# A column sum over 32,768 rows: the tile scheduler's ring against a hand-synchronised ring with loops

## Chip, cores and metric

The kernel runs on one core of one Trainium2 chip. The metric is the device time of one execution in microseconds; the time of the kernel before is the median of seven runs. A profile of one further execution gives the instructions of each engine, the DMA packets with their start, length and size, and every landing of a transfer. VectorE (DVE in the profile), TensorE (PE, with PEld for its weight loads), ScalarE (ACT), GpSimd (POOL) and SyncE (SP) are the engines; 16 DMA engines move the data. All times here are microseconds unless marked ns.

## The reference

```python
def setup_inputs():
    batch, seq, dim = 32, 1024, 2048
    return {"grad_output": np.random.randn(batch, seq, dim).astype(np.float32)}

def reference(grad_output):
    return np.sum(grad_output, axis=(0, 1)).astype(np.float32)
```

The input is 32,768 rows of 2,048 float32, which is 268.4 MB; the output is one row of 2,048. The work is one addition for each number that is read.

## The kernel before

The input is seen as 32,768 rows. They are taken in blocks of 128 x m rows: partition p gets m neighbouring rows, so that a block is m "single rows" of 128 partitions x 2,048 columns, 1 MB each, and 256 single rows make up the input. Below, a row is such a single row. A load of m rows takes from each partition one contiguous piece of m x 8 KB.

Three buffers matter. `ring` has room for 24 rows (192 KB of each partition), `head` for one, and `ones` is a column of ones with which a matmul sums over the partitions. PSUM holds the sums, one bank for each piece of columns: three pieces of 512 (`LEFT`) and two of 256 (`RIGHT`). The third number of a piece is the group of 32 partitions in which its sum stands: 1, 2 and 3 for the left pieces, 0 and 1 for the right ones. `add` (lines 65 to 71) issues one matmul for each piece of a row.

`PLAN` (line 14) is the list of the loads: 27 tiles of 8 rows, then 7, 6, 6, 5, 4, 2, -2, 2, -2. For a positive number VectorE adds. It first adds the running sum to the new tile (line 114), then folds the tile (line 93): a tile of 8 rows is folded to 4 while fewer than 23 tiles have been added (`N_WIDE`, `WIDE`), and to a single row behind that, by halving. For a negative number the rows are not folded: TensorE sums them straight into PSUM (lines 104 to 107). Behind the last positive tile stand three filler matmuls into a bank of their own (line 120). Then the running sum goes to PSUM (line 121).

`LAST` = (2, 1) are the last three rows. They are loaded in two halves of columns, first the left 1,536 columns of both loads, then the right 512, into a place of their own, and TensorE sums them with the stop flag on the last (lines 125 to 133). Lines 134 to 138 copy the five sums from PSUM to `res`, which lies in `head`: ScalarE the pieces 0, 2 and 4, VectorE 1 and 3. Line 139 sends `res` out.

All loads are issued by SP (line 85), one after the other in the order of the program. A load into a place of the ring waits until the last reader of that place is done; these waits, and all others between engines, are put in by the tile framework. The places follow one another in the ring and start again at 0 when a tile doesn't fit behind the last one; for the tiles of 8 that makes three places.

Lines 51 and 52 issue 60 drains on VectorE at the start of its program. Line 53 sets `ones`, line 54 is a copy on ScalarE that has no use but to load its table.

Of the kernel before, what the change touches and what calls it, by code (L numbers as in the profile page):

```python
# [1 line left out]

# [4 lines left out]

P = 128
RING = 24  # L10

PLAN = (8,) * 27 + (7, 6, 6, 5, 4, 2, -2, 2, -2)
LAST = (2, 1)

N_WIDE = 23
WIDE = 4
DRAINS = 60
FILLERS = 3  # L20

LEFT = ((0, 512, 1), (512, 512, 2), (1024, 512, 3))
RIGHT = ((1536, 256, 0), (1792, 256, 1))


@with_exitstack
def kernel(
    ctx: ExitStack,
    tc: tile.TileContext,
    grad_output: bass.AP,  # L30
    out: bass.AP,
):
    nc = tc.nc
    fp32 = mybir.dt.float32
    D = out.shape[-1]
    flat = grad_output.rearrange("b s d -> (b s) d")
    R = flat.shape[0]
    assert (1 + sum(abs(m) for m in PLAN) + sum(LAST)) * P == R

    const_pool = ctx.enter_context(tc.tile_pool(name="const", bufs=1))  # L40
    psum_pool = ctx.enter_context(tc.tile_pool(name="psum", bufs=1, space=bass.MemoryType.PSUM))

    ring = const_pool.tile([P, RING * D], fp32)
    head = const_pool.tile([P, D], fp32)
    ones = const_pool.tile([P, 1], fp32)
    warm = const_pool.tile([1, 1], fp32)
    res = head[0:1, :]

    for _ in range(DRAINS):
        nc.vector.drain(fusable=False)
    nc.gpsimd.memset(ones[:], 1.0)  # L53
    nc.scalar.copy(out=warm[:], in_=ones[0:1, :])  # L54

    sums = {}
    for b, (lo, n, g) in enumerate(LEFT + RIGHT):
        bank = psum_pool.tile([P, 512], fp32, tag=f"ps{b}", name=f"ps{b}")  # L60
        sums[lo] = bank[32 * g : 32 * g + 1, :n]
    junk = psum_pool.tile([P, 512], fp32, tag="junk", name="junk")
    started = set()

    def add(at, pieces, base=0, stop=False):
        for lo, n, g in pieces:
            x = at + lo - base
            nc.tensor.matmul(  # L68
                sums[lo], lhsT=ones[:], rhs=ring[:, x : x + n], start=(lo not in started), stop=stop
            )  # L70
            started.add(lo)

    row = pos = 0

    def take(m):
        nonlocal pos
        if pos + m > RING:
            pos = 0
        at = pos
        pos += m  # L80
        return at

    def load(first, m, dst, lo=0, hi=D):
        src = flat[first : first + P * m].rearrange("(p m) d -> p m d", p=P)[:, :, lo:hi]
        nc.sync.dma_start(out=dst.rearrange("p (m d) -> p m d", m=m), in_=src)  # L85

    def rows(at, m):
        return ring[:, at * D : (at + m) * D]

    def fold(at, height, to):  # L90
        while height > to:
            k = min(height - to, height // 2)
            nc.vector.tensor_add(out=rows(at, k), in0=rows(at, k), in1=rows(at + height - k, k))  # L93
            height -= k

    load(row, 1, head[:])
    row += P
    run = height = None
    n_fold = 0
    for m in PLAN:  # L100
        at = take(abs(m))
        load(row, abs(m), rows(at, abs(m)))
        row += P * abs(m)
        if m < 0:
            for j in range(-m):
                add((at + j) * D, LEFT + RIGHT)
            continue
        to = min(m, WIDE if n_fold < N_WIDE else 1)
        if n_fold == 0:
            nc.vector.tensor_add(out=rows(at, 1), in0=rows(at, 1), in1=head[:])  # L110
        else:
            to = min(to, height)
            fold(run, height, to)
            nc.vector.tensor_add(out=rows(at, to), in0=rows(at, to), in1=rows(run, to))  # L114
        n_fold += 1
        fold(at, m, to)
        run, height = at, to
        if n_fold == sum(m > 0 for m in PLAN):
            for _ in range(FILLERS):
                nc.tensor.matmul(junk[0:1, :], lhsT=ones[:], rhs=rows(at + m - 1, 1)[:, :512], start=True, stop=True)  # L120
    add(run * D, LEFT + RIGHT)

    at = take(sum(LAST)) * D
    cut = RIGHT[0][0]
    for lo, hi, pieces in ((0, cut, LEFT), (cut, D, RIGHT)):
        first = row
        for i, m in enumerate(LAST):
            n = hi - lo
            load(first, m, ring[:, at : at + m * n], lo, hi)
            first += P * m  # L130
            for j in range(m):
                add(at, pieces, base=lo, stop=(i == len(LAST) - 1 and j == m - 1))
                at += n
    for k, (lo, n, g) in enumerate(LEFT + RIGHT):
        if k in (0, 2, 4):
            nc.scalar.copy(out=res[:, lo : lo + n], in_=sums[lo])  # L136
        else:
            nc.vector.tensor_copy(out=res[:, lo : lo + n], in_=sums[lo])  # L138
    nc.sync.dma_start(out=out[None, :], in_=res)


# [1 line left out]
_INS = ['grad_output']  # L143
_OUTS = [((2048,), 'float32')]


# [23 lines left out]
```

## Time and profile before

| what | value |
|---|---|
| median of 7 runs | 630.68 |
| all runs | 630.46, 630.62, 630.64, 630.68, 630.69, 631.35, 631.50 |
| the profiled execution's own time | 631.31 |
| its span, first to last instruction | 629.2 |
| VectorE busy | 544.0 (86%), 89 instructions |
| TensorE busy | 16.7 (3%), 86 instructions |
| DMA, over the span | 268.46 MB, 427 GB/s |
| packets | 6164 |
| 8-row loads, issue to landing, median | 29.9 |
| the output row's issue | 626.32 |

The span is what the profile's clock shows between the first and the last instruction; the device time is 2.1 longer in the profiled execution. The busy share of an engine is an average over the whole span. "Idle before" in a group of instructions is the time for which its engine stood still just ahead of them, with what ended it. The chain of waits is followed back from the last instruction: at each step to what released it, or to the instruction before it on its engine.

### The profile page before, as it was taken

To read this page: it belongs to the slowest core of one execution; us is meant where nothing else is said; L and a number is where in the kernel's file an instruction comes from. 1 tells how busy PE (TensorE), PEld (TensorE's weight loads), DVE (VectorE), ACT (ScalarE), POOL (GpSimd) and SP (SyncE) were. 2 spreads that over 40 slices of the span, in tenths; PEclk is the share of its full clock that TensorE was granted. 3 is DMA by queue.
4 is the path that set the end of the run, shared out by engine and by line. 5 is a ranking of instruction groups with operands and counts; after the bars stand their busy time and mean duration, and the time that the engine had idled before them with its cause. 6 is when DMAs were issued, how large, how long until landed. Compare 5 with 4: busy or idle time off the path is not lost.

```text
span 629.2 us, 484 instructions
## 1 busy us (share of the span) xinstructions
PE 16.7 (3%) x86; PEld 3.7 (1%) x86; DVE 544.0 (86%) x89; ACT 3.0 (0%) x5; POOL 0.3 (0%) x5
## 2 busy tenths in 40 slices
PE   0000000000000000000000000000000000000046
PEld 0000000000000000000000000000000000000001
DVE  0349888889888898888998888988899999999994
ACT  0000000000000000000000000000000000000000
POOL 0000000000000000000000000000000000000000
PEclk9999999999999999999999999999999999999998
DMA  9999999999999999999999999999999999999995
GB/s 400 417 450 417 450 417 450 421 446 425 442 425 442 429 437 433 433 437 429 442 425 450 417 454 412 454 412 458 408 458 408 458 408 433 430 447 406 426 427 231
DMA packets 6164, 268.46 MB, mean 427 GB/s; under 512 B 657, under 2 KB 657, under 8 KB 1425
## 3 DMA queue, kind: packets, MB, share of 16 engines
q1 hardware_dynamic: 6162, 268.45, 98.8%
q14 instruction: 2, 0.02, 0.0%
HBM read 268.44 MB, written 0.01 MB: 427 GB/s over the span
## 4 chain that ended last, share of the span: by engine, by line
DMA 60%; DVE 37%; PE 2%; issue 0%; another core or an unknown queue 0%; SPq 0%; ACT 0%; DVEq 0%
DMA ring<-in_grad_output_dram 60%; DVE ring L114 19%; DVE ring L93 18%; PE ps L68 2%; SPq L85 0%; ACT head L136 0%; DVEq L114 0%
## 5 line engine op out<-in xcount | busy, mean ns | idle before, releaser
L93 DVE TENSOR_TENSOR ring<-ring 128x8192 f32<-128x8192 f32 (+3 forms) x53 | 324.1, 6116 | 1.8
L114 DVE TENSOR_TENSOR ring<-ring 128x8192 f32<-128x8192 f32 (+1 forms) x33 | 216.4, 6559 | 49.7 <-DMA ring<-in_grad_output_dram 49.3
L68 PE MATMUL ps<-ring,ones 128*1 128x512 f32 (+1 forms) x80 | 13.9, 647 | 608.9 <-DMA ring<-in_grad_output_dram 608.9
L110 DVE TENSOR_TENSOR ring<-ring,head 128x2048 f32<-128x2048 f32 x1 | 2.3, 2293 | 25.4 <-DMA ring<-in_grad_output_dram 25.4
L68 PEld LDWEIGHTS ps<-ring,ones 128*1 128x1 f32 x80 | 3.2, 89 | 619.5 <-issue 615.3
L138 DVE COPY head<-ps 1x512 f32<-1x512 f32 (+1 forms) x2 | 1.1, 548 | 5.1 <-PE ps L68 5.1
L136 ACT COPY head<-ps 1x512 f32<-1x512 f32 (+1 forms) x3 | 1.5, 507 | 622.6 <-PE ps L68 622.4
L120 PE MATMUL junk<-ring,ones 128*1 128x512 f32 x6 | 2.7, 592 | 0.4 <-DMA ring<-in_grad_output_dram 0.4
L54 ACT ACT_TABLE_LOAD x1 | 1.3, 1283 | 0.7 <-PEq L154 0.7
L120 PEld LDWEIGHTS junk<-ring,ones 128*1 128x1 f32 x6 | 0.4, 83 | 2.3 <-issue 1.4
L54 ACT COPY warm<-ones 1x1 f32<-1x1 f32 x1 | 0.2, 191 | 0.0
L154 POOL MEMSET const-bfloat16-1.0<- 128x1 bf16 x1 | 0.1, 103 | 0.0
L154 POOL MEMSET const-uint8-127<- 128x1 uint8 x1 | 0.1, 103 | 0.0
L53 POOL MEMSET ones<- 128x1 f32 x1 | 0.1, 100 | 0.3 <-POOLq L154 0.3
L154 POOL MEMSET const-float32-0.0<- 128x1 f32 x1 | 0.1, 99 | 0.2 <-issue 0.2
L154 POOL MEMSET const-float32-1.0<- 128x1 f32 x1 | 0.1, 99 | 0.0
## 6 DMA issues: line engine op xcount, KB each, us to landing
ring<-in_grad_output_dram SPq DMA_DIRECT2D x2, 6144.0 KB, 27.1
ring<-in_grad_output_dram SPq DMA_DIRECT2D x4, 2048.0 KB, 32.3
ring<-in_grad_output_dram SPq DMA_DIRECT2D x1, 7168.0 KB, 32.0
ring<-in_grad_output_dram SPq DMA_DIRECT2D x1, 5120.0 KB, 37.1
ring<-in_grad_output_dram SPq DMA_DIRECT2D x1, 4096.0 KB, 31.5
ring<-in_grad_output_dram SPq DMA_DIRECT2D x1, 1536.0 KB, 27.7
head<-in_grad_output_dram SPq DMA_DIRECT2D x1, 1024.0 KB, 4.8
ring<-in_grad_output_dram SPq DMA_DIRECT2D x1, 768.0 KB, 28.9
```

The lines of the kernel that those rows point to most:

```text
L53: nc.gpsimd.memset(ones[:], 1.0)
L54: nc.scalar.copy(out=warm[:], in_=ones[0:1, :])
L68: nc.tensor.matmul(sums[lo], lhsT=ones[:], rhs=ring[:, x : x + n], start=(lo not in started), stop=stop)
L93: nc.vector.tensor_add(out=rows(at, k), in0=rows(at, k), in1=rows(at + height - k, k))
L110: nc.vector.tensor_add(out=rows(at, 1), in0=rows(at, 1), in1=head[:])
L114: nc.vector.tensor_add(out=rows(at, to), in0=rows(at, to), in1=rows(run, to))
L120: nc.tensor.matmul(junk[0:1, :], lhsT=ones[:], rhs=rows(at + m - 1, 1)[:, :512], start=True, stop=True)
L136: nc.scalar.copy(out=res[:, lo : lo + n], in_=sums[lo])
L138: nc.vector.tensor_copy(out=res[:, lo : lo + n], in_=sums[lo])
L154: nc = _bacc.Bacc("TRN2", target_bir_lowering=False, num_devices=1)
```

## The change

The kernel no longer leaves its waits to the framework. The whole body stands in a critical section, and each wait and each count of a semaphore is written out.

The ring becomes three slots of 8 rows. There are 30 tiles of 8 rows, all folded by VectorE alike: wait for the slot, add the four rows of the sum before to the tile, count `vec` up, fold 8 rows to 4. A `drain` stands in front of each addition. Behind the first tile VectorE runs a loop of nine laps with three tiles in each, one for each slot; two more tiles follow the loop, and behind the last one the sum is folded to one row, and `end` is counted up twice on the way.

The load of tile k waits for `vec` to reach k - 2. SP still issues all loads in the order of the list.

Behind the tiles come 13 rows that TensorE sums alone. The first goes to row 3 of slot 0, the other twelve in turn to rows 0, 1 and 2 of it (three "lanes"); the first row of each lane waits for tile 28's addition, and from then on a load waits until the row that was in its lane has been summed (`used`). TensorE runs a loop of four laps with three rows in each; ahead of each row stands one filler matmul of 256 columns into a bank of its own. Then it sums the running sum (when `end` is 2), and the last rows.

`LAST` becomes (1, 1): two rows, again in a left and a right half, into the upper half of slot 2, which is free when `end` is 1. The 60 drains at the start and the three fillers are gone. The copies of the sums and the output are as before, with written waits.

```diff
-RING = 24
-PLAN = (8,) * 27 + (7, 6, 6, 5, 4, 2, -2, 2, -2)
-LAST = (2, 1)
-N_WIDE = 23
+SLOTS = 3
+TILE = 8
+TILES = 30
 WIDE = 4
-DRAINS = 60
-FILLERS = 3
+DIRECT = 13
+LAST = (1, 1)
+LOOPS = 9
+LANES = 3
+FILLER = 256
...
+    load(1, head[:], head_in)
+    for k in range(TILES):
+        s = k % SLOTS
+        load(TILE, rows(s * TILE, TILE), slot_in[s], (vec, k - 2) if k >= SLOTS else None)
+    load(1, rows(LANES, 1), row_in[LANES], (vec, TILES - 2))
+    for i in range(DIRECT - 1):
+        j = i % LANES
+        load(1, rows(j, 1), row_in[j], (used, i - LANES + 1) if i >= LANES else (vec, TILES - 2))
+    cut = RIGHT[0][0]
+    final = []
+    at = (SLOTS * TILE - WIDE) * D
+    for lo, hi, pieces in ((0, cut, LEFT), (cut, D, RIGHT)):
+        first = at_row
+        for m in LAST:
+            lane = last_in[len(final)]
+            n = m * (hi - lo)
+            load(m, ring[:, at : at + n], lane, (end, 1), first, lo, hi)
...
+    def issue(dst, src, lane, after):
+        dma = nc.sync.dma_start(out=dst, in_=src)
+        if after is not None:
+            dma._wait_ge(*after)
+        dma.then_inc(lane, 16)
+
+    section = tc.tile_critical(no_gpsimd_drain=True)
+    section.__enter__()
+    for x in loads:
+        issue(*x)
...
-    for _ in range(DRAINS):
+    def take(engine, lane):
+        engine.wait_ge(lane, 16).then_inc(lane, -16)
+
+    def vadd(at, other, n):
+        return nc.vector.tensor_add(out=rows(at, n), in0=rows(at, n), in1=other)
+
+    def settle():
         nc.vector.drain(fusable=False)
+
+    def fold(at, n):
+        return vadd(at, rows(at + n, n), n)
+
+    def tile_sum(s):
+        at, before = s * TILE, (s - 1) % SLOTS * TILE
+        take(nc.vector, slot_in[s])
+        settle()
+        vadd(at, rows(before, WIDE), WIDE).then_inc(vec, 1)
+        settle()
+        return fold(at, WIDE)
+
+    take(nc.vector, slot_in[0])
+    fold(0, WIDE)
+    nc.vector.wait_ge(head_in, 16)
+    settle()
+    vadd(0, head[:], 1)
+    with nc.vector.Fori(0, LOOPS):
+        for s in (1, 2, 0):
+            tile_sum(s)
+    tile_sum(1)
+    tile_sum(2).then_inc(end, 1)
+    at = (SLOTS - 1) * TILE
+    settle()
+    fold(at, 2)
+    settle()
+    fold(at, 1).then_inc(end, 1)
...
+    nc.tensor.wait_ge(one, 1)
+    add(LANES * D, LEFT + RIGHT, wait=(row_in[LANES], 16), start=True)
+    with nc.tensor.Fori(0, (DIRECT - 1) // LANES):
+        for j in range(LANES):
+            take(nc.tensor, row_in[j])
+            if FILLER:
+                nc.tensor.matmul(
+                    psum[0:1, 5 * 512 : 5 * 512 + FILLER], lhsT=ones[:], rhs=ring[:, j * D : j * D + FILLER], start=True, stop=True
+                )
+            add(j * D, LEFT + RIGHT, used=used)
+    add((SLOTS - 1) * TILE * D, LEFT + RIGHT, wait=(end, 2))
+    for f, (at, m, lo, hi, pieces, lane) in enumerate(final):
+        for j in range(m):
+            stop = f % len(LAST) == len(LAST) - 1 and j == m - 1
+            add(at + j * (hi - lo), pieces, lo, wait=None if j else (lane, 16), stop=stop)
...
+    nc.sync.dma_start(out=out[None, :], in_=res)._wait_ge(cp, len(ready)).then_inc(done, 16)
+    nc.sync.wait_ge(done, 16)
+    section.__exit__(None, None, None)
```

## The prediction

> **What bounds the kernel now.** I read the page first, slices and queues, then the chain of waits over the end of the span, then the shapes of the vector engine's work, then the tail by clock window.
>
> ```profile
> span 629.2 us, 484 instructions
> ...
> DMA  9999999999999999999999999999999999999995
> ...
> q1 hardware_dynamic: 6162, 268.45, 98.8%
> q14 instruction: 2, 0.02, 0.0%
> ```
>
> The input queue (q1) keeps the 16 DMA engines busy for 98.8% of 629.2, that is 621.6 us. Only 7.6 us are no transfer: 1.8 at the front, 5.3 behind the last landing, and the rest in an uneven start and finish. No change that moves the same bytes can win more than part of that.
>
> ```profile
> 578.72 0.33 SPq L85
> ...
> 579.58 36.68 DMA ring<-in_grad_output_dram
> 616.25 0.04 issue
> 616.29 9.61 PE ps L68 x43
> 625.90 0.02 issue
> 625.93 0.36 ACT head L136
> ```
>
> This is the end of the chain of waits: a landing at 616.25, then 9.6 us of TensorE without a gap, a ScalarE copy, the output. So TensorE sets the end. The landing records of the last load show why this matters: fifteen DMA engines finish it by 623.05, the sixteenth at 623.86, yet the last matmul ends at 625.90 and the output is issued at 626.32.
>
> ```profile
> L93 DVE TENSOR_TENSOR ring<-ring 128x8192 f32<-128x8192 f32 x27 | 234.7, 8692 | 0.9
> L114 DVE TENSOR_TENSOR ring<-ring 128x8192 f32<-128x8192 f32 x22 | 191.2, 8692 | 49.3 <-DMA ring<-in_grad_output_dram 49.3
> L93 DVE TENSOR_TENSOR ring<-ring 128x4096 f32<-128x4096 f32 x8 | 35.4, 4426 | 0.3
> L93 DVE TENSOR_TENSOR ring<-ring 128x2048 f32<-128x2048 f32 x15 | 34.4, 2293 | 0.5
> ...
> L136 ACT COPY head<-ps 1x512 f32<-1x512 f32 x2 | 1.2, 578 | 622.4 <-PE ps L68 622.4
> ...
> L136 ACT COPY head<-ps 1x256 f32<-1x256 f32 x1 | 0.4, 363 | 0.1
> ```
>
> The shapes give the prices: a wide tile is 2 x 8.69 = 17.4 us of VectorE against the 19.36 between landings of 8-row tiles (45.08 and 64.42, for instance). VectorE waits 49 us in all, inside the wide stretch; from 451 on the chain is its work without a pause, and its last fold (2.29 us, begun at 617.51) ends at 619.80.
>
> ```profile
> 613.30:616.75 3.45, 1.29 (x10) 0.13 (x9) 3.42 (x2) 0.00 (x0) 0.00 (x0) 1.00 0.95 398
> 616.75:620.16 3.41, 3.41 (x21) 0.65 (x18) 3.02 (x2) 0.00 (x0) 0.00 (x0) 0.50 1.00 412
> 620.16:623.57 3.41, 3.41 (x29) 0.94 (x30) 0.00 (x0) 0.00 (x0) 0.00 (x0) 1.00 0.68 257
> 623.57:627.00 3.43, 2.32 (x19) 0.67 (x11) 1.10 (x2) 1.52 (x3) 0.00 (x0) 1.00 0.00 0
> ```
>
> The first figures are the length and TensorE's busy time, and the third from the end is its clock. After a stretch with 1.29 of 3.45 us busy it is halved for 3.41 us, and then full.
>
> **What a row costs on TensorE.** Each matmul call is two passes (40 calls stand as x80). At full clock 512-column passes start 0.43 us apart, at half clock 0.85. Passes to different output partitions start within 20 ns of each other, so they overlap; the partition that takes a 512 and a 256 piece sets the row: 2 x 0.43 + 2 x 0.215 = 1.29 us, and 2.56 at half clock.
>
> **How this execution stands to the median.** It took 631.31 (2.15 around its span), 0.63 over the median. I replay its tail at full clock: the run's row starts at 619.87 and ends at 621.16, three left rows (0.86 each) at 623.73, three right rows (0.43 each) at 625.02, and 0.16 of latency gives 625.18 instead of 625.90, 0.72 less. The seven runs fall into five at 630.46 to 630.69 and two at 631.35 and 631.5. That gap of about 0.7 fits, so I take this execution for one of the slower group and the median for a tail at full clock.
>
> **The change, part by part.**
>
> *Bytes and packets.* The packet records give 2421 ns for 64 KB, 309 for 8 KB, 615 for 16 KB, 239 for 6 KB, 86 for 2 KB. Per engine, before: 621.25 us. After: 30 tiles x 8 x 2.421 = 581.04, head and 13 single rows 14 x 8 x 0.309 = 34.61, last pieces 16 x 0.239 + 16 x 0.086 = 5.20, 48 semaphore writes x 0.009 = 0.44; 621.29. So +0.04: larger tiles pay for the smaller rows.
>
> *Code fetch.* One 8 KB packet of the instruction queue runs at 29.2 us, when VectorE has passed 60 drains and its first adds. Landings spread by 0.04 between the last two engines before it and by 0.84 ever after: one engine is 0.80 late to the end. Afterwards VectorE holds 51 instructions, not 191, fewer than the 66 or so it had passed at that fetch, so none is expected: -0.80. If the loop fetches once, 0; more often is a rival below.
>
> *Loop and drains on VectorE.* Drains at line 52 start 0.04 apart. Two waits or drains of 0.04 per add and a back edge, bounded between the page's smallest gap (0.02) and 1.0, stay inside the spare 3 x (19.36 - 17.4) = 5.9 us per lap. Cost nothing; without that cover, 9 laps x at most 1.0. Load k still waits for the wide add of tile k-2, some 10.6 us before the transfer in front of it ends.
>
> *The end of VectorE's work.* The last tile lands with 13 rows still to come, 13 x 2.47 = 32.1 us; its 8.69 + 8.69 + 4.43 + 2.29 = 24.1 are done before. So VectorE leaves the end of the chain.
>
> *Start.* SP gets a semaphore step and a branch ahead of its first load: 0.08 us from barrier to issue now, so between 0 and 0.3; taken 0.12. All loads move with it.
>
> *Single rows.* A lane's buffer is loaded again after its row is summed. Landing to needed start of the next transfer is two other rows, 4.94 us. Against it: 0.08 to start, 1.45 row, 0.1 semaphore, 0.33 issue, 1.03 from issue to first packet (0.73 to 1.76 at the start) = 3.0, at half clock 4.3. So the stream is not starved. The filler sits in its own partition group and overlaps. Behind the row loads SP has only the last four pieces.
>
> *Tail.* From the last landing F: row 11 lands at F-5.2, the left pieces at F-3.29 and F-1.38. At full clock row 11 and the run's row end at F-2.5, the second left piece at F-0.28. ScalarE then copies 0.58 + 0.58, ending F+0.92, and the last 256 piece (done at F+0.67) by F+1.32; output issue F+1.35. If the clock is halved in the last window, up to 0.7 more. Busy 1.29 of 2.47 us is between 1.29 of 3.45 (halved next) and 2.32 of 3.43 (kept); I add 0.1.
>
> *End.* Output issue to the span's end is 2.85 now. One more exchange with all engines (a barrier round is 0.16 in the trace), but the two SP waits with a 0.45 pause (627.86 to 628.31) go: -0.45 to +0.3; taken 0.
>
> **Sum.** F = 623.05 + 0.04 + 0.12 + 0.04 = 623.25; output issue 624.60 against 626.32, or 1.72 less; with the 0.1, 1.62. 631.31 - 1.62 = 629.69, so 629.7. Against the median, which I take to have the 0.7 already, it is 1.0 less: 0.16%, inside the 0.2% (1.26 us) that a measurement of this kernel can tell from no change.
>
> **Two rules weighed.** After the fetch row above: the Trainium skill, "Runtime: NRT & Kernel Launch", section "Instruction fetch mechanics", says that a taken branch to code outside a two-page window must fetch by DMA first, and that kernels therefore prefer unrolling. That speaks against this change; no run here shows a loop yet. If every VectorE edge did so, the sum would be the fetch rival's below. After the clock rows: "TensorE: Matmul & The Clock Gate", section "HAM oscillation — how this bites in real kernels", holds that idle gaps under about 3.4 us keep the clock; this trace disagrees, since gaps of 0.4 and 2.16 us in one window were enough to halve it. By the rule the 0.1 above would be 0.
>
> **Rivals.**
> - *Forecast, 0.46:* about 1.0 less, 629.7, own range 629.4 to 630.6.
> - *Faster, 0.33:* the 0.63 of this execution is not the clock but profiling, so the median also ends 1.7 later than it need; or the end exchange is shorter. 630.68 - 1.7 = 629.0. For it: one profile only, two runs of seven in the slower group. Against: the replay fits the gap.
> - *Slower, code fetches, 0.12:* each back edge of VectorE's loop fetches 8 KB through the same DMA engine, 0.80 each: 9 edges give 629.7 + 7.2 = 636.9. It decides from three fetches (2.4 - 1.0 is over 1.26). Against: 17 instructions a lap, well short of the place where before fetched.
> - *Three lanes too few, 0.09:* the isolated 1 MB load took 4.8 us; with a row at half clock and its steps 4.8 + 2.72 + 0.2 = 7.7 against 3 x 2.47 = 7.4, 0.3 a lap, 0.9 in three laps: 630.6. At 0.75 a lap it would be slower than before; split 0.04 no change, 0.05 slower.
>
> **How the numbers follow.** Faster 0.33; no change 0.46 + 0.04 = 0.50; slower 0.12 + 0.05 = 0.17. The range 628.6 to 631.8 takes in the end's -0.45, the faster case and the lane case with a halved tail, and leaves out the fetches.
>
> **What would show it.** Right: no instruction packet between 1 and 620 us; the last load landing on all 16 engines within 0.1 us, near 623.3; the chain ending in DMA, a few matmuls, a copy; DMA share as now. Wrong: fetches at VectorE's laps and one engine ever later; DMA idle in the last 35 us; a TensorE chain of several microseconds behind the last landing; first loads later than 1 us.

## The result, and the profile after

The changed kernel takes 633.55 us (median of 13 runs), the kernel before 630.62 (33 runs); the ratio is 1.0037, with a 95% interval of 1.0026 to 1.0049. So it is slower. And the executions scatter: 630.01 to 636.10, where before keeps within 630.36 to 631.54. The profiled execution took 629.98, less than any of the 13; it alone would have told the opposite. Why the executions of one kernel differ so is what the experiments ask.

Page of the changed kernel, the span, DMA busy in slices, and the queues (packets, MB, share):

```profile
span 628.2 us, 676 instructions
...
DMA  9999999999999999999999999999999999999896
...
q1 hardware_dynamic: 6914, 268.45, 99.1%
q14 instruction: 1, 0.00, 0.0%
```

The DMA engines stay busy, and no 8 KB code packet is left. The chain of waits at the end of the same execution (start, duration, what):

```profile
613.92 8.78 DMA ring<-in_grad_output_dram
622.70 0.04 issue
622.74 1.08 PE psum L162 x6
623.82 0.56 ACT head L192
624.37 0.02 issue
624.40 0.58 ACT head L192
624.98 0.02 issue
625.00 0.36 ACT head L192
```

This is the end that was forecast: a landing, one short piece of TensorE, three ScalarE copies. The 9.6 us of TensorE are gone. So the profiled execution shows a gain, and most others lose 2 to 6 us that it doesn't show. The question for the experiments was where.

### The profile page after: what moved, and what is told of

It is laid out like the page before. It is cut to its first block, busy times and chain, and to the rows that moved or that the text cites. A ratio compares the mean times of both kernels' runs of the same rounds, so it can differ in the third digit from the quotient of the medians.

```text
span 628.2 us, 676 instructions
## 1 busy us (share of the span) xinstructions
PE 24.2 (4%) x184; PEld 5.9 (1%) x184; DVE 522.9 (83%) x64; ACT 3.0 (0%) x5; POOL 0.3 (0%) x5
## 5 line engine op out<-in xcount | busy, mean ns | idle before, releaser
L120 DVE TENSOR_TENSOR ring<-ring 128x8192 f32<-128x8192 f32 (+2 forms) x61 | 519.6, 8517 | 88.9 <-DVEq L117 86.1
L162 PE MATMUL psum<-ring,ones 128*1 128x512 f32 (+1 forms) x160 | 24.1, 530 | 588.9 <-DMA ring<-in_grad_output_dram 588.9
L162 PEld LDWEIGHTS psum<-ring,ones 128*1 128x1 f32 x160 | 5.5, 82 | 600.7 <-DMA ring<-in_grad_output_dram 590.8
L178 PE MATMUL psum<-ring,ones 128*1 128x256 f32 x24 | 7.2, 380 | 11.5 <-PEq L117 11.5
L192 ACT COPY head<-psum 1x512 f32<-1x512 f32 (+1 forms) x3 | 1.5, 507 | 621.5 <-PE psum L162 621.4
L178 PEld LDWEIGHTS psum<-ring,ones 128*1 128x1 f32 x24 | 1.4, 80 | 17.5 <-issue 17.5
```

What stands on the lines that cost most here:

```text
L120: return nc.vector.tensor_add(out=rows(at, n), in0=rows(at, n), in1=other)
L162: mat = nc.tensor.matmul(sums[lo], lhsT=ones[:], rhs=ring[:, x : x + n], start=start, stop=stop)
L178: nc.tensor.matmul(psum[0:1, 5 * 512 : 5 * 512 + FILLER], lhsT=ones[:], rhs=ring[:, j * D : j * D + FILLER], start=True, stop=True)
L192: copy(out=res[:, lo : lo + n], in_=sums[lo])._wait_ge(mm, ready[lo]).then_inc(cp, 1)
```

## The experiments

Each experiment ran beside the kernel before on the same chip. In the order of what they tell:

| kernel | median (lowest to highest), runs | ratio to before, 95% interval |
|---|---|---|
| changed, again | 633.71 (632.69 to 635.17), 6 | 1.0038 (1.0025 to 1.0050) |
| both loops written out | 635.16 (633.10 to 635.91), 5 | 1.0057 (1.0040 to 1.0074) |
| no filler | 633.27 (630.33 to 636.53), 10 | 1.0036 (1.0017 to 1.0054) |
| TensorE warm beforehand | 631.33 (629.89 to 633.11), 10 | 1.0012 (1.0000 to 1.0023) |
| warm, longer rows | 632.23 (630.74 to 633.55), 6 | 1.0031 (1.0019 to 1.0043) |
| six lanes | 630.71 (630.65 to 630.88), 10 | 0.9997 (0.9987 to 1.0006) |
| six lanes, no filler | 629.76 (629.64 to 630.08), 11 | 0.9984 (0.9975 to 0.9993) |
| four lanes | 629.82 (629.66 to 630.29), 11 | 0.9985 (0.9976 to 0.9994) |
| four lanes, reload held back | 632.07 (629.92 to 635.94), 10 | 1.0020 (1.0000 to 1.0040) |
| four lanes, longer rows | 630.37 (630.19 to 630.80), 10 | 0.9991 (0.9981 to 1.0000) |

### The changed kernel again: where the time goes

> The changed kernel unchanged, to see whether its spread (630.0 to 636.1, median 633.6, in the runs shown) comes again and to profile one more execution; the kernel before spreads over 1.2 us only. All theories: 630 to 636 again. What each expects of a slow profile: (clock) single rows on TensorE that take 2.5 us and more where the fast profile has 1.47; (loops) instruction packets in the span and one DMA engine ever later; (lanes) DMA idle between single-row loads although rows take 1.47.

Its profiled execution took 635.17. TensorE's timeline over the single rows (start, time, line, shape; in brackets the idle time before, here ended by TensorE's own wait for a landing at line 117):

```profile
588.80 2.72 PE L162 MATMUL psum<-ring,ones 128*1 128x512 f32 x10 [588.80 <-DMA ring<-in_grad_output_dram]
...
592.18 1.92 PE L162 MATMUL psum<-ring,ones 128*1 128x256 f32 x7
...
594.64 1.06 PE L162 MATMUL psum<-ring,ones 128*1 128x256 f32 x7
...
596.35 0.38 PE L178 MATMUL psum<-ring,ones 128*1 128x256 f32 x1 [0.64 <-PEq L117]
...
599.13 0.38 PE L178 MATMUL psum<-ring,ones 128*1 128x256 f32 x1 [1.33 <-PEq L117]
...
603.23 0.38 PE L178 MATMUL psum<-ring,ones 128*1 128x256 f32 x1 [2.64 <-PEq L117]
...
611.68 0.59 PE L178 MATMUL psum<-ring,ones 128*1 128x256 f32 x1 [2.04 <-PEq L117]
...
621.14 0.38 PE L178 MATMUL psum<-ring,ones 128*1 128x256 f32 x1 [3.01 <-PEq L117]
```

and the same view of the changed kernel's first profiled execution, the one of 629.98:

```profile
591.92 1.02 PE L162 MATMUL psum<-ring,ones 128*1 128x256 f32 x7
...
593.91 0.38 PE L178 MATMUL psum<-ring,ones 128*1 128x256 f32 x1 [0.96 <-PEq L117]
...
596.40 0.38 PE L178 MATMUL psum<-ring,ones 128*1 128x256 f32 x1 [1.04 <-PEq L117]
...
598.88 0.38 PE L178 MATMUL psum<-ring,ones 128*1 128x256 f32 x1 [1.02 <-PEq L117]
```

In the one of 629.98 TensorE waits about 1.0 ahead of each row, and rows follow 2.48 apart. In the one of 635.17 it waits up to 3.0: the data are late. In both the first row starts cold (2.72). In the execution of 635.17 full clock comes at 594.61 and not at 591.61 (the seven passes of 256 columns that end the second row take 1.92 there and 1.02 in the other). So two rows and the start of a third run at half clock, from 588.80 on. The first reload, that is the first load into a lane whose earlier row has been summed, is therefore issued at 594.13 in place of 592.98.

The windows 606 to 616 (length, busy time of PE, PEld, DVE, ACT and POOL, then TensorE's clock, DMA share, GB/s), the execution of 635.17:

```profile
606.00:616.00 10.00, 6.95 (x48) 1.75 (x40) 4.75 (x2) 0.00 (x0) 0.00 (x0) 0.83 0.94 338
```

and the one of 629.98:

```profile
606.00:616.00 10.00, 5.83 (x48) 1.55 (x48) 4.79 (x2) 0.00 (x0) 0.00 (x0) 1.00 1.01 422
```

The queue moves 338 GB/s instead of 422 at a DMA share that is only 0.07 lower. The packet records tell most of why: with 8 KB packets of 0.31 as the rule, 129 of some 1,660 packets took over 60 ns more, up to 1.03 more. Together that is 48.8, or 3.0 on each of the 16 engines. From its landing of the first single row to that of the last piece an engine takes 38.9 on average here and 34.9 in the one of 629.98. So longer packets are about three quarters of what an engine loses; the lower DMA share stands for the rest. Landings of one row spread over 2.68 among the 16 DMA engines (0.61 at most in the one of 629.98), and a row can only start behind the slowest. TensorE mostly waits for data here. Its clock falls again (611.68 to 615.09 and 621.92 to 625.33, half clock in the clock record); the row that starts at 611.68 is then summed 1.3 later than at full clock, and the reload behind it (614.44) again comes only 2.1 before its turn. The last landing is at 628.87, not 623.99.

### The loops

> Both loops written out, all else as in the changed kernel. Loop theory (a back edge costs in some executions): the spread shrinks to about 1 us and the median falls to 630 to 631, one code fetch (0.8) included. Clock and lane theories: spread and median stay, 632 to 635.

```diff
-    with nc.vector.Fori(0, LOOPS):
+    for _ in range(LOOPS):
...
-    with nc.tensor.Fori(0, (DIRECT - 1) // LANES):
+    for _ in range((DIRECT - 1) // LANES):
```

635.16: no better, and the scatter stays. The loops are not the cause. The longer code brings back an 8 KB code packet, at 261.55, and from then on one engine lands 0.75 behind the other fifteen.

### Six lanes

> Six lanes for the single rows in place of three, so that a row's buffer is loaded again only after five other rows (12.4 us) and not two (4.9 us). Lane theory (a late row starves the DMA queue): median 630 or below with a spread under 1.5 us, even if some rows run at half clock. Loop theory: no change, 632 to 635. Clock theory without lanes (TensorE alone is too slow at the end): at most 1 us less, 632 to 634.

```diff
-LANES = 3
+LANES = 6
```

630.71, with a spread of 0.23 over ten runs. That takes 3 us and the scatter away; more lanes are all that was changed (TensorE's loop then has two laps). What was left over: a 16 KB code packet at 622.8, and the last load landing at 624.96 on one engine and by 623.77 on the other fifteen.

### The filler

> No filler matmuls beside the single rows; TensorE has less to do while it waits. Clock theory: TensorE is halved more often, so the median rises, 634 to 637, and rows of 2.5 us appear. Loop and lane theories (with the clock of no account): median stays within 1 us of the changed kernel's.

```diff
-FILLER = 256
+FILLER = 0
```

633.27, the same scatter. The median doesn't rise, so the clock theory by itself fails here. The filler buys nothing that can be measured: a row takes 1.45 without it and 1.46 with it.

### Four lanes, and six without the filler

> Four lanes in place of three, three laps; 24 more TensorE instructions than the changed kernel, 48 fewer than with six lanes. The slow profiles of the unchanged kernel show the first reload of a lane issued 2.1 and 1.8 us before its turn, the fast one 3.3; a fourth lane adds 2.47 to each. Lane theory: spread under 1 us and median 629.6 to 630.3, below the six-lane kernel's 630.7 because that one's code fetch of 16 KB at 622.8 (1.2 us on one DMA engine) is gone. If three or fewer rows in flight are still too few: spread of 2 us and more, median over 631.

> Six lanes and no filler. Lane theory: the filler does nothing that the lanes need, spread under 1 us, median 629.6 to 630.5 (24 fewer TensorE instructions than with six lanes and the filler, so no code fetch near the end). Clock theory by itself: TensorE falls to half clock between rows and the last rows run late, 631 to 633.

```diff
-LANES = 3
+LANES = 4
```

629.82 and 629.76, spreads of 0.63 and 0.44. Both beat before, by 0.15% and 0.16%. The window 606 to 616 of the four-lane kernel:

```profile
606.00:616.00 10.00, 5.83 (x48) 1.55 (x48) 4.82 (x2) 0.00 (x0) 0.00 (x0) 1.00 1.02 424
```

The loads' lines of the DMA view (issues, KB each, median time from issue to landing), with three lanes, the execution of 635.17:

```profile
ring<-in_grad_output_dram SPq DMA_DIRECT2D x13, 1024.0 KB, 7.4
```

the one of 629.98:

```profile
ring<-in_grad_output_dram SPq DMA_DIRECT2D x13, 1024.0 KB, 6.1
```

and with four lanes:

```profile
ring<-in_grad_output_dram SPq DMA_DIRECT2D x13, 1024.0 KB, 8.3
```

This median alone doesn't tell a good execution from a bad one. With four lanes it is longer than in the good execution with three, because a load stands in the queue while others run; in the bad one with three it is longer because the loads themselves are slow. My reading of the six-lane kernel's extra 0.9 as its code fetch is not shown: without the filler the same 16 KB packet runs at 622.88, and all engines land by 623.82.

### Is it the cold start, or the lateness?

> Three lanes as in the changed kernel, but twelve junk matmuls of 512 columns run just ahead of the first single row, so that TensorE is at full clock when it lands. Theory (a cold start makes the first reload late, the queue runs dry and doesn't recover): spread falls to 1.5 us or less, median 629.8 to 631. If the three lanes fail at full clock too: spread and median as in the changed kernel, 632 to 635.

```diff
+    nc.tensor.wait_ge(head_in, 16)
+    nc.tensor.wait_ge(vec, TILES - 2)
+    with nc.tensor.Fori(0, WARM):
+        nc.tensor.matmul(psum[0:1, 5 * 512 : 6 * 512], lhsT=ones[:], rhs=head[:, :512], start=True, stop=True)
```

with WARM = 12. The median falls to 631.33 but the spread stays at 3.2, more than the 1.5 expected. By the ratios to before (1.0012, against 1.0038 on another chip) the cold start is the larger part, not all: two runs of 630.8 had full clock over the whole span and are still 0.9 behind the best, and others lost more.

> As the one before, and the filler is 512 columns in the group of the longest partition, so that every row takes 0.86 more (2.3 in place of 1.47) at full clock, still less than the 2.48 between landings. Theory: each reload is issued about 2.4 us before its turn and the queue runs dry without any half clock, median 633 to 637. If only the clock matters, not when the reload is issued: as the one before, under 631.

As the one before, with FILLER = 512 written to `psum[32:33]`. The median rises by 0.9 to 632.23, less than expected, and the intervals of the two ratios still touch (1.0000 to 1.0023 and 1.0019 to 1.0043), so it is likely, but not shown, that the longer rows cost more. All six runs have a clock of 0.999 or 1.000 over the span, and yet reach 633.55. So a half clock is not needed for the loss.

> Four lanes, but each reload waits for one row more than it needs (used is asked to be one higher), so that it is issued as late as with three lanes, about 3.3 us before its turn in place of 5.8, and two rows are in flight. Theory (what counts is how early the reload is issued, not the buffer or the code): the spread of several microseconds is back, median 632 to 635, and lengthened 8 KB packets are back. If the number of buffers or the loop's form counts: as four lanes, 629.8 with a spread under 1 us.

```diff
-        load(1, rows(j, 1), row_in[j], (used, i - LANES + 1) if i >= LANES else (vec, TILES - 2))
+        load(1, rows(j, 1), row_in[j], (used, i - LANES + 2) if i >= LANES else (vec, TILES - 2))
```

with LANES = 4. Same buffers and code as four lanes; only the reload is issued a row later. The scatter is back: 629.92 to 635.94. The median of 632.07 is at the low end of what was expected.

> Four lanes with a cold start and a filler of 512 columns in the group of the longest partition, so that each row takes 2.3 us at full clock and over 4 at half clock: a worse clock and slower rows than the changed kernel has. Theory: reloads are still issued 3 us and more before their turn once TensorE is at full clock, median 629.8 to 631.5. If slow rows in themselves cost the time: 633 to 637.

Four lanes with FILLER = 512 in `psum[32:33]`, cold start. TensorE stands still for 0.2 at most ahead of a row from 588.84 to 624.93, and the kernel still takes 630.37 with a spread of 0.61. It ran on the same chip as the one before, which scatters over 6.0.

The profiled executions in one table. "Ahead" is the time from a reload's issue to the landing of the load in front of it (first reload; median of the others); the packets are those of 8 KB that took over 60 ns longer than 312.

| kernel, its profiled execution | ahead, first | ahead, others | lengthened packets | last landing |
|---|---|---|---|---|
| changed, 629.98 | 3.29 | 3.36 | 3 | 623.99 |
| changed, 635.17 | 2.08 | 4.33 | 129 | 628.87 |
| loops written out, 635.41 | 2.51 | 4.41 | 118 | 629.44 |
| no filler, 631.60 | 3.29 | 3.76 | 20 | 625.54 |
| warm, 629.89 | 3.36 | 3.35 | 4 | 623.91 |
| warm, longer rows, 630.74 | 2.52 | 2.50 | 20 | 624.29 |
| four lanes, held back, 631.04 | 3.35 | 3.35 | 8 | 624.75 |
| four lanes, longer rows, 630.46 | 4.69 | 4.98 | 0 | 623.68 |
| four lanes, 629.75 | 5.20 | 5.84 | 0 | 623.75 |
| six lanes, 630.66 | 10.05 | 10.82 | 0 | 624.96 |
| six lanes, no filler, 629.79 | 9.60 | 10.81 | 0 | 623.82 |

Where the first reload is 4.7 or more ahead, not one packet is lengthened. Where it is 3.4 or less ahead, some always are, and whether the execution gets away with them differs from run to run. Once engines are out of step, the later reloads look early only because the slowest engine is late. That holds for the first one of the written-out loops too: the 2.51 is counted to the engine that the code packet made late, and to the other fifteen it is 1.8. This is the 1.8 in what was expected of four lanes; it belongs to that kernel and not to the unchanged one.

## Why the prediction was wrong

The step that failed is *Single rows*: "So the stream is not starved." It counted 0.08 + 1.45 + 0.1 + 0.33 + 1.03 = 3.0 against 4.94. The first three terms hold: a row takes 1.46 from its start, and the next reload is issued 3.3 to 3.4 ahead, as 4.94 - 1.63 has it. What the step mis-sized is the rest, the lead that a load needs: 0.33 + 1.03 = 1.36, where 1.03 from issue to first packet came from the empty queue at the start. Into a running queue 3.4 isn't reliably enough, and 4.7 is; no run lies between. The held-back reload shows that it is the lead: with four lanes, the same buffers and the same code, a lead of 3.35 in place of 5.2 to 5.8 brought the scatter back. No run separates the time of the lead from the packets that still stand in the queue (at 0.31 each, 3.4 is 11 on each engine and 4.7 is 15). And why packets take longer behind a late issue stays open. The step also treated the 16 engines as one. Each has its own share of every row and a landing is the slowest one's, so one late packet delays the next reload for all of them; that this is how the loss grows is my reading of the spread landings.

The half clock entered the same step as 4.3, "not starved" too. By its own terms that is a lead of 4.94 - 2.94 = 2.0, and 2.1 was measured where TensorE stayed cold longest; again only the need was too small. How long TensorE stays cold differs by execution (full clock came at 591.6 and at 594.6), and with it the first reload's lead (3.3 and 2.1). The prediction saw the halving in the trace of before, but gave it a price in the tail alone, 0.1.

The rival "three lanes too few" had the place. Its price was wrong: 0.3 a lap from one isolated load, 0.9 in all, against 3 in the median and up to 6. At that price it could not cross to the slower side, and 0.09 was too low.

The rest held:
- *Code fetch:* gone, and with it the 0.80; the written-out loops bring it back (0.75).
- *Loop and drains on VectorE:* cost nothing. Back edges take 0.06 on VectorE, 0.21 to 0.22 on TensorE, under cover, and bring no fetch. The rival with a fetch at each edge is out. The Trainium skill, "Runtime: NRT & Kernel Launch", section "Instruction fetch mechanics", names a fetch only for a taken branch whose target lies outside the two pages that are held; the runs agree, with no 8 KB instruction packet in nine laps.
- *End of VectorE's work, tail:* output issue 1.40 behind the last landing, forecast 1.35. *End:* 2.81, forecast 2.85.
- *Filler:* it overlaps, as forecast, though not in a group of its own: group 0 holds a right piece too.
- *Start:* first load at 0.945, 0.21 later than before (forecast 0.12). The last landing came at 623.99 instead of 623.25: 0.09 is the start, 0.25 one engine late since 606 (a lengthened packet), 0.16 rows 2.485 apart instead of 2.472; 0.24 is unexplained.
- *The median against the profiled execution of before:* the runs beside the experiments bear it out; executions of before with a clock of 1.000 have spans near 628.4, those with 0.997 near 629.2.

Without the starvation the sum comes close, partly by luck: four lanes take 629.82, forecast 629.7. In their profiled execution the output is issued at 625.16, where the sum with its 0.1 has 624.70. Against that, the time around the span is 1.78 (1.7 to 2.4 in the eleven runs) where before has 2.15, which was not foreseen and was not followed up.

## What to carry to other kernels

When a buffer is loaded again only after its data are used, count how long before its turn the load is issued, and compare that with a lead that the queue is seen to keep up with (here 4.7 us held and 3.4 didn't, with 1 MB loads), not with the latency of a load into an empty queue. One good profile doesn't clear a kernel whose runs scatter: profile again until one shows the loss, and look at the spread of one load's landings over the DMA engines. Where a lane waits for TensorE, take its half clock for the first turn.

## What the hardware showed that was not expected

- A row's landing spread over the 16 DMA engines is 0.2 to 0.7 while the queue is ahead and no code packet has run, and up to 2.7 (the execution of 635.17) and 3.3 (loops written out) with lengthened packets; the engines did not fall back into step within 25 us.
- TensorE at 1.46 busy of 2.48, and at 1.45 without a filler, kept full clock for 37 us (591.56 to 629.11, without a filler). Before, 1.29 of 3.45 halved it. The clock record changes in steps of 3.41, and the windows of that length in the execution of 635.17 show what decides:

```profile
601.44:604.85 3.41, 1.46 (x12) 0.39 (x12) 3.32 (x2) 0.00 (x0) 0.00 (x0) 1.00 1.01 423
...
608.27:611.68 3.41, 1.37 (x12) 0.30 (x10) 2.48 (x2) 0.00 (x0) 0.00 (x0) 1.00 0.87 329
611.68:615.09 3.41, 3.41 (x21) 1.00 (x23) 0.00 (x0) 0.00 (x0) 0.00 (x0) 0.50 0.94 356
```

The first has a gap of 2.64 ahead of its row and full clock behind it; the second has a gap of 2.04 and half clock behind it. In the twelve profiles together, 127 such windows stand at full clock. Each of the 17 with at most 1.37 busy (12 of them at the end of the work) was followed by half clock, and each of the 110 with at least 1.45 by full clock. So in these traces it is the busy time in a window that counts, not the longest gap. The rule weighed in the prediction (the Trainium skill, "TensorE: Matmul & The Clock Gate", section "HAM oscillation — how this bites in real kernels"), that idle gaps matter from about 3.4 on, fits neither the tail of before nor this execution.
